# Dilated attention with keys and copied queries held by position class, weights' sums from a ones column

## The chip, the cores and the metric

One core of a Trainium2 chip runs the whole program. The metric is the device time of one execution in microseconds, the median of several runs. TensorE is called PE here (its weight loads PEld), VectorE DVE, ScalarE ACT, GpSimd POOL, and SyncE, which issues the DMAs, SP.

## The reference, cut to what matters

Two transformer blocks follow each other on one sequence of 1024 positions of width 1024. The change lies in the second block's dilated attention: 8 heads of 64 values. Three branches of a softmax over a window of keys are mixed by their denominators, which is one softmax over the keys of all three with those of several branches counted once for each.

```python
DILATED_BRANCHES = ((128, 1), (512, 4), (2048, 16))
...
def dilated_attention(q, k, v, rel_bias):
    outs, lses = [], []
    for window, dil in DILATED_BRANCHES:
        o, l = dilated_window_branch(q, k, v, rel_bias, window, dil)
        ...
    w = jax.nn.softmax(jnp.stack(lses, axis=0), axis=0)
    return jnp.einsum('ibsh,ibshd->bshd', w.astype(q.dtype), jnp.stack(outs, axis=0))
```

The kernel joins the branches with dilation 4 and 16: all their keys have the query's position modulo 4. That is the class piece; the window of dilation 1 is the band piece.

## The kernel before, in words

Values are float32; a matmul operand is split into a high and a low part, and a product is made as high by high, low by high and high by low. In the second block the stages follow each other: values and gates, then the qk stage (queries and keys), then 16 class pieces, then 16 band pieces, and from the fourteenth band piece on the groups of the output projection (`wp_group`).

**The qk stage.** `d_run` makes each block product and hands it to `qk_evac` with its number p and one of four head pairs s. Order of p: 2, 1, 5, 6, 3, 7, 4. Pieces 1 and 4 are the first and second half of the queries, 3 and 7 of the keys; 2, 5, 6 are partial products. `key_operand` (L1239) stores a head pair's keys from an SBUF tile f: ACT casts the high parts (L1247), DVE subtracts for the low ones (L1250), ACT casts a second copy (L1251); positions lie one after another. `query_operand` (L1225) does the same for queries by ACT L1233 and DVE L1236, for piece 4 out of PSUM.

**A piece.** `dil_quad` (L1805) is a generator for four heads and 128 queries. It makes scores (`scores`: four matmuls of 128 rows at L1263, four of 64 at L1268), takes the minimum of bias minus score per query on DVE (L1831) and the exponential on ACT with its sum read out (L1834); after a yield it transposes (PE L1842) and copies out of PSUM (ACT L1845, DVE L1847); after another it multiplies by the values (L1861) and copies the result out (DVE L1863). A class piece (class c, query half qb) reads queries and keys with a step of 4 elements and stores its result, minima and sums into `cls_d` in DRAM. A band piece loads that back (`xc`, L1822) and joins the two by minima and sums (DVE L1870 to L1876, ACT L1872, POOL L1877 to L1881), then transposes the result (PE L1887) and splits it (ACT L1889, DVE L1890).

**What sets the order.** Each `pump` starts one new generator and then steps the older ones, the youngest first. So PE does the scores of piece k, the transposes of k-1 and the products with the values of k-2. Each engine works in program order. `self.low = nc.gpsimd` puts the splits of the output weights (`wl`, L281) on POOL during the band stage. Values for the class pieces (`vc`, four DMAs), for the band (`vb`, nine) and the band's bias (`bb`, two) are loaded on SP between the stages, and each DMA waits for the one eight before it.

Of the kernel before, what the change touches and what calls it, by code (L numbers as in the profile page):

```python
# [10 lines left out]
F32 = mybir.dt.float32  # L11
F32R = mybir.dt.float32r
AF = mybir.ActivationFunctionType
# [162 lines left out]
class Kern:  # L176
# [1062 lines left out]
    def key_operand(self):  # L1239

        nc = self.nc
        k = [self.S("kst", dt=F32R) for _ in range(3)]
        def put(h, ps):
            sl = slice(512 * h, 512 * h + 512)
# [9 lines left out]
    def scores(self, sc, qs, ks, q0, k0, step, nk):  # L1254


        nc = self.nc
        qc = slice(q0 % 512, q0 % 512 + step * (P - 1) + 1, step)
        kc = slice(k0, k0 + step * (nk - 1) + 1, step)
        th = q0 // 512  # L1260
        for j in range(2):
            for s in range(2):
                nc.tensor.matmul(sc[s][:, 256 * j : 256 * j + nk], qs[j][th][:, s, qc], ks[j][s][:, kc],  # L1263
                                 start=(j == 0), stop=False, skip_group_check=True)
        for j in range(2):
            for s in range(2):
                pr = slice(64 * s, 64 * s + 64)
                nc.tensor.matmul(sc[s][:, 256 * j : 256 * j + nk], qs[j][th][pr, s, qc], ks[j][2][pr, kc],  # L1268
                                 start=False, stop=(j == 1), skip_group_check=True)


    def att1_quad(self, n, u, aq, ak, av, att):
# [6 lines left out]
        self.scores(sc, aq[2 * u : 2 * u + 2], [ak, ak], n * P, k0, 1, nk)  # L1279
# [168 lines left out]
    def block2(self, Z, x2_d):  # L1448
# [75 lines left out]
        def vc_load(c):  # L1524
            t = self.S("vc", [P, 2, 512])
            nc.sync.dma_start(t, vsrc[c].rearrange("(b p) c -> p b c", p=P))
            vc.append(t)

        vc, cb = [], []
        cls_d = dp.tile([SEQ, 2, 264], F32, name="cls_d")  # L1530
        qs, ks, kput = [None] * 4, [None] * 4, [None] * 4
        qput = [None] * 4
        cls = [self.dil_quad("c", (c, qb), u, qs, ks, vc, cb, cls_d)
# [3 lines left out]
        def qk_evac(p, s, ps):  # L1537
            th, ch = self.OUT[p]
            if p in (2, 5, 6):
                nc.scalar.copy(self.part(p, s), ps)  # L1540
                return
            src = ps
            if p != 4:
                src = self.H("f")
                nc.vector.tensor_tensor(src, ps, self.part(p, s), ALU.add)
            if ch == 0:
                if p == 1:
                    qs[s], qput[s] = self.query_operand()
                qput[s](th, src)
            else:  # L1550
                if p == 3:
                    ks[s], kput[s] = self.key_operand()
                kput[s](th, src)
            if p == 7 and s == 0:
                vc_load(0)
                cb.extend(self.bias_load(0, 384, "cb", range(4)))
            if p == 4 and s == 0:
                for c in range(1, 4):
                    vc_load(c)
            if p == 4 and s == 3:  # L1560
                self.pend.extend(cls)
# [5 lines left out]
        cb += self.bias_load(0, 384, "cb", range(4, 8))  # L1567

# [3 lines left out]
        vb = [self.S("vb", [P, 2, 512]) for _ in range(5)]  # L1572
        for m in range(9):
            lo, hi = max(0, P * m - 64), min(SEQ, P * m + 64)
            nc.sync.dma_start(vb[m // 2][0 : hi - lo, m % 2, :], v_d[lo:hi, :])
        bb = self.bias_load(L_CLS, 256, "bb")
        while self.pend:
            self.pump()

# [225 lines left out]
    def dil_quad(self, kind, where, u, qs, ks, vt, bias, cls_d, MX=None):  # L1805

        nc = self.nc
        if kind == "c":
            c, qb = where
            q0, k0, step, nk, b0 = c + 512 * qb, c, 4, 256, 128 - 128 * qb  # L1810
            segs = [(0, P, vt[c][:, 0, :]), (P, P, vt[c][:, 1, :])]
            co = self.H("co", [P, 264])
        else:
            n = where
            lo, hi = max(0, P * n - 64), min(SEQ, P * n + 192)
            q0, k0, step, nk, b0 = n * P, lo, 1, hi - lo, lo - (P * n - 64)
            segs = []
            for m in (n, n + 1):
                a0, a1 = max(0, P * m - 64), min(SEQ, P * m + 64)
                segs.append((a0 - lo, a1 - a0, vt[m // 2][0 : a1 - a0, m % 2, :]))  # L1820
            x2 = self.S("xc", [P, 2, 264])
            nc.sync.dma_start(x2[:, 0, :], cls_d[n * P : n * P + P, u, :])  # L1822
            co = x2[:, 1, :]
        sc = [self.PS("sc") for _ in range(2)]
        self.scores(sc, qs[2 * u : 2 * u + 2], ks[2 * u : 2 * u + 2], q0, k0, step, nk)
        z = self.S("z", [P, 4, 256])
        for s in range(2):
            for j in range(2):
                h, x = 4 * u + 2 * j + s, 2 * j + s
                nmc = co[:, 256 + x : 257 + x]  # L1830
                nc.vector.tensor_tensor_reduce(  # L1831
                    out=z[:, x, :nk], in0=sc[s][:, 256 * j : 256 * j + nk], in1=bias[h][:, b0 : b0 + nk], scale=-0.125,
                    scalar=BIG, op0=ALU.add, op1=ALU.min, accum_out=nmc)
                nc.scalar.activation(z[:, x, :nk], z[:, x, :nk], AF.Exp, bias=nmc, scale=-1.0,  # L1834
                                     accum_out=co[:, 260 + x : 261 + x])
        yield
        pT = self.S("pT", [P, 8, P])
        for g in range(2):
# [4 lines left out]
            if kind == "c" or segs[0][1] == segs[1][1]:  # L1843
# [14 lines left out]
        for x in range(4):  # L1858
            h = 4 * u + x
            for e, (o, w, vv) in enumerate(segs):  # L1860
                nc.tensor.matmul(pv[:, 64 * x : 64 * x + 64], pT[0:w, 2 * x + e, :], vv[:, 64 * h : 64 * h + 64],  # L1861
                                 start=(e == 0), stop=(e == 1))
# [5 lines left out]
        d, e = (self.mp.tile([P, 2, 4], F32, tag="d2", name=self.nm("d2"), bufs=6) for _ in range(2))  # L1868
        mn, rc = self.M("mn", 4), self.M("rc", 4)
        nc.vector.tensor_tensor(mn, x2[:, 0, 256:260], x2[:, 1, 256:260], ALU.min)  # L1870
        nc.vector.tensor_tensor(d, mn[:, None, :].to_broadcast([P, 2, 4]), x2[:, :, 256:260], ALU.subtract)
        nc.scalar.activation(e, d, AF.Exp)  # L1872
        yield
        nc.vector.tensor_tensor(d, e, x2[:, :, 260:264], ALU.mult)
        nc.vector.tensor_tensor(rc, d[:, 0, :], d[:, 1, :], ALU.add)
        nc.vector.reciprocal(rc, rc)  # L1876
        nc.gpsimd.tensor_tensor(e, e, rc[:, None, :].to_broadcast([P, 2, 4]), ALU.mult)  # L1877
        for i in range(2):
            v = x2[:, i, 0:256].rearrange("p (h d) -> p h d", d=64)
            nc.gpsimd.tensor_tensor(v, v, e[:, i, :, None].to_broadcast([P, 4, 64]), ALU.mult)  # L1880
        nc.gpsimd.tensor_tensor(co[:, 0:256], co[:, 0:256], x2[:, 0, 0:256], ALU.add)  # L1881
        yield
# [3 lines left out]
        for j in range(2):  # L1886
            nc.tensor.transpose(tp[:, j, :], co[:, P * j : P * j + P], self.ident)  # L1887
        hi, lo = (z[:, :, (n % 4) * P : (n % 4) * P + P] for z in MX.pair(u, n // 4))
# [35 lines left out]
```

## Time and profile before

| | us |
|---|---|
| median of 3 runs (lowest to highest) | 2574.4 (2571.2 to 2575.66) |
| the profiled execution's own time | 2574.72 |
| its span | 2572.9 |
| busy PE / DVE / ACT / POOL in the span | 2504.7 / 1765.6 / 1142.2 / 178.7 |
| qk stage ends, class stage, band stage (start to end in the span) | 1681; 1683.7 to 1756.5; 1756.5 to 1861 |

Times of a trace row count from the start of the span. Busy shares are averages over stages with different limits; what bounds a stretch is read from the chain of waits in it.

### The profile page before, as it was taken

How to read it: one execution, taken by the hardware profiler on the slowest of the kernel's cores; microseconds unless marked ns; L12 is line 12 of the kernel's file. 1: busy time of each engine (PE TensorE's matmuls, PEld its weight loads, DVE VectorE, ACT ScalarE, POOL GpSimd, SP SyncE). 2: the span in 40 equal slices, each digit the busy share in tenths (PEclk: the TensorE clock that was granted, in tenths of full speed). 3: DMA queues.
4: the chain of work that ended last, by engine and by line, in shares of the span. 5: the costliest groups of instructions: out<-in, count | busy, mean ns of one | idle time of the engine just before them, and what ended most of it. 6: DMA issues, size and time to landing. Idle time of an engine off the chain costs nothing.

```text
span 2572.9 us, 31324 instructions
## 1 busy us (share of the span) xinstructions
PE 2504.7 (97%) x11857; PEld 2073.0 (81%) x11857; DVE 1765.6 (69%) x2789; ACT 1142.2 (44%) x2068; POOL 178.7 (7%) x236
## 2 busy tenths in 40 slices
PE   7999999999999999999999999999999999899998
PEld 5888888888787888878788777888887888788886
DVE  7664456556899755555799986666558444478888
ACT  5444445412425433333333644566436555553334
POOL 1000000000002000000000300002421000000006
PEclk9999999999999999999999999999899999999999
DMA  4333333135343122233433415221242333522334
GB/s 157 104 110 103 123 103 107 39 113 185 109 186 131 66 70 87 87 130 98 174 121 131 144 49 172 102 81 51 81 160 82 104 117 103 180 108 81 115 123 147
DMA packets 178703, 291.57 MB, mean 113 GB/s; under 512 B 10168, under 2 KB 84552, under 8 KB 178552
## 3 DMA queue, kind: packets, MB, share of 16 engines
q1 hardware_dynamic: 178552, 289.57, 33.1%
q8 instruction: 93, 1.52, 0.2%
q14 instruction: 58, 0.48, 0.1%
HBM read 212.89 MB, written 80.31 MB: 114 GB/s over the span
## 4 chain that ended last, share of the span: by engine, by line
PE 78%; DVE 13%; DMA 3%; ACT 3%; issue 2%; POOL 1%; SPq 0%; DVEq 0%; ACTq 0%; POOLq 0%
PE da L1201 6%; PE a L500 6%; PE a L502 6%; PE a L501 6%; PE da L1200 6%; PE da L1199 6%; PE db L1201 3%; PE db L1200 3%; PE db L1199 3%; PE b L502 3%; PE b L501 3%; PE b L500 3%; DVE wl L281 3%; PE pv L1861 2%; DVE midl L281 2%
## 5 line engine op out<-in xcount | busy, mean ns | idle before, releaser
L500 PE MATMUL a<-midh,ws 128*128 128x512 f32 x708 | 276.8, 391 | 9.1 <-DVE f L1669 8.0
L502 PE MATMUL a<-midh,ws 128*128 128x512 f32 x708 | 276.4, 390 | 0.0
L501 PE MATMUL a<-midl,ws 128*128 128x512 f32 x708 | 276.4, 390 | 0.0
L1201 PE MATMUL da<-wh,midl 128*128 128x512 f32 x624 | 245.1, 393 | 6.6 <-DVE midl L281 6.6
L1200 PE MATMUL da<-wl,midh 128*128 128x512 f32 x624 | 244.6, 392 | 3.4 <-DVE wl L281 3.4
L1199 PE MATMUL da<-wh,midh 128*128 128x512 f32 x624 | 246.0, 394 | 0.6 <-ACT midh L279 0.6
L279 ACT CAST midh<-mt 128x1024 fp32r<-128x1024 f32 x80 | 82.9, 1036 | 244.6 <-DVE mt L1142 81.3
L1201 PE MATMUL db<-wh,midl 128*128 128x512 f32 x436 | 171.0, 392 | 3.5 <-DVE midl L281 3.5
L1200 PE MATMUL db<-wl,midh 128*128 128x512 f32 x436 | 170.8, 392 | 2.2 <-DVE wl L281 2.2
L1199 PE MATMUL db<-wh,midh 128*128 128x512 f32 x436 | 171.1, 392 | 1.4 <-ACT midh L279 1.4
L500 PEld LDWEIGHTS a<-midh,ws 128*128 128x128 f32 x708 | 133.4, 188 | 38.7 <-issue 8.9
L501 PEld LDWEIGHTS a<-midl,ws 128*128 128x128 f32 x708 | 133.5, 189 | 27.7
L502 PEld LDWEIGHTS a<-midh,ws 128*128 128x128 f32 x708 | 133.5, 189 | 27.7
L279 ACT CAST ws<-tc 128x512 fp32r<-128x512 f32 x180 | 111.4, 619 | 88.3 <-DVE tc L414 87.1
L1201 PEld LDWEIGHTS da<-wh,midl 128*128 128x128 f32 x624 | 117.8, 189 | 34.5 <-DVE midl L281 10.3
L1200 PEld LDWEIGHTS da<-wl,midh 128*128 128x128 f32 x624 | 117.9, 189 | 29.0 <-DVE wl L281 4.8
L500 PE MATMUL b<-midh,ws 128*128 128x512 f32 x360 | 140.1, 389 | 0.0
L501 PE MATMUL b<-midl,ws 128*128 128x512 f32 x360 | 140.1, 389 | 0.0
L502 PE MATMUL b<-midh,ws 128*128 128x512 f32 x360 | 140.0, 389 | 0.0
L279 ACT CAST wh<-raw 128x1024 fp32r<-128x1024 f32 x121 | 120.6, 1037 | 42.0 <-DMA raw<-in_w_ff_dram 15.2
L1199 PEld LDWEIGHTS da<-wh,midh 128*128 128x128 f32 x624 | 118.0, 189 | 26.0 <-issue 1.2
L281 DVE TENSOR_TENSOR wl<-raw,wh 128x1024 fp32r<-128x1024 f32 x117 | 136.2, 1197 | 3.6 <-ACT wh L279 3.5
(348 smaller groups left out, 5822.8 us busy)
## 6 DMA issues: line engine op xcount, KB each, us to landing
raw<-in_w_ff_dram SPq DMA_DIRECT2D x31, 1024.0 KB, 5.4
mid_d<-f SPq DMA_DIRECT2D x108, 256.0 KB, 2.1
midr<-mid_d SPq DMA_DIRECT2D x52, 512.0 KB, 6.9
raw<-in_w_in_dram SPq DMA_DIRECT2D x22, 1024.0 KB, 5.4
x<-x_d SPq DMA_DIRECT2D x24, 512.0 KB, 4.5
raw<-in_w_up_dram SPq DMA_DIRECT2D x11, 1024.0 KB, 5.6
raw<-in_w_gate_dram SPq DMA_DIRECT2D x10, 1024.0 KB, 5.5
xt<-in_x_dram SPq DMA_DIRECT2D x16, 512.0 KB, 10.9
```

The source lines that it names most:

```text
L279: self.nc.scalar.copy(hi, s)
L281: e.tensor_tensor(lo, s, hi.bitcast(F32), ALU.subtract)
L500: nc.tensor.matmul(ps, hi[:, i], xh, start=(first and i == 0), stop=False, skip_group_check=True)
L501: nc.tensor.matmul(ps, hi[:, i], xl, start=False, stop=False, skip_group_check=True)
L502: nc.tensor.matmul(ps, lo[:, i], xh, start=False, stop=(i == 3), skip_group_check=True)
L1199: nc.tensor.matmul(ps, xh, wh, start=(kt == 0 and p in (1, 5, 2)), stop=False, skip_group_check=True)
L1200: nc.tensor.matmul(ps, xh, wl, start=False, stop=False, skip_group_check=True)
L1201: nc.tensor.matmul(ps, xl, wh, start=False, stop=(kt == m - 1), skip_group_check=True)
L1861: nc.tensor.matmul(pv[:, 64 * x : 64 * x + 64], pT[0:w, 2 * x + e, :], vv[:, 64 * h : 64 * h + 64], start=(e == 0), stop=(e == 1))
```

## The change

Keys and a second copy of the queries are stored grouped by position modulo 4 (class by class). A class piece then reads both without a step; a band piece reads its 256 keys as eight runs of 32, so its columns stand by class, and its value tiles and bias are brought into that order too. The first and last band piece of each half use two groups of columns instead of one: 16 matmuls instead of 8, 8 minima instead of 4. Each head's 64 values get a 65th column of ones, so that a product with the weights also gives their sum; the exponential no longer reads a sum. A band piece starts its minimum from the class piece's, so the class part is scaled by one exponential and added. The class result's copy out of PSUM moves from DVE to ACT.

```diff
-    def key_operand(self):
+    def key_operand(self, r=1):
...
+            w = 512 // r
+            v = [x.rearrange("p (r j) -> p r j", r=r)[:, :, w * h : w * h + w] for x in k]
+            ps = ps.rearrange("p (j r) -> p r j", r=r)
             for s in range(2):
                 pr = slice(64 * s, 64 * s + 64)
-                nc.scalar.copy(k[s][pr, sl], ps[pr, :])
+                nc.scalar.copy(v[s][pr], ps[pr])
             for s in range(2):
...
-                nc.vector.tensor_tensor(k[2][pr, sl], ps[pr, :], k[s][pr, sl].bitcast(F32), ALU.subtract)
-                nc.scalar.copy(k[s][po, sl], ps[pr, :])
+                nc.vector.tensor_tensor(v[2][pr], ps[pr], v[s][pr].bitcast(F32), ALU.subtract)
+                nc.scalar.copy(v[s][po], ps[pr])
...
+        def vb_load(u, m):
+            lo, hi = max(0, 32 * m - 16), min(256, 32 * m + 16)
+            v, w = v_slot("vb", vb, u, m), hi - lo
+            for c in range(4):
+                nc.sync.dma_start(
+                    v[c * w : c * w + w], vsrc[c, lo:hi, 256 * u : 256 * u + 256].rearrange("p (h d) -> p h d", d=64))
...
                 qput[s](th, src)
+                qc[s][th] = t = self.S("qc", [P, 2, 512], F32R)
+                for i in range(2):
+                    nc.scalar.copy(t[:, i, :].rearrange("p (r j) -> p r j", r=4),
+                                   qs[s][th][:, i, :].rearrange("p (j r) -> p r j", r=4))
...
+            if step == 10:
+                for m in range(9):
+                    vb_load(0, m)
+            if step in (11, 12):
+                h = 4 * (step - 11)
+                b, t = self.bias_load(L_CLS, 256, "bn", range(h, h + 4)), self.S("bb", [P, 4, 256])
+                for i in range(4):
+                    nc.gpsimd.tensor_copy(t[:, i, :].rearrange("p (g r j) -> p g r j", g=2, r=4),
+                                          b[i].rearrange("p (g j r) -> p g r j", g=2, r=4))
...
+                if i == 4:
+                    for m in range(9):
+                        vb_load(1, m)
...
             nc.sync.dma_start(x2[:, 0, :], cls_d[n * P : n * P + P, u, :])
+            yield
...
+                nm = co[:, 260 + x : 261 + x]
+                least = BIG if kind == "c" else x2[:, 0, 260 + x : 261 + x]
+                for o, w, fb, fz in parts:
+                    nc.vector.tensor_tensor_reduce(
+                        out=fz(z[:, x, o : o + w]), in0=fz(sc[s][:, 256 * j + o : 256 * j + o + w]), in1=fb(bias[h]),
+                        scale=-0.125, scalar=least, op0=ALU.add, op1=ALU.min, accum_out=nm)
+                    least = nm
+                nc.scalar.activation(z[:, x, :nk], z[:, x, :nk], AF.Exp, bias=nm, scale=-1.0)
+        if kind == "b":
...
+            nc.gpsimd.tensor_tensor(d, co[:, 260:264], x2[:, 0, 260:264], ALU.subtract)
+            nc.scalar.activation(d, d, AF.Exp)
+            v = x2[:, 0, 0:260].rearrange("p (h d) -> p h d", d=65)
+            nc.gpsimd.tensor_tensor(v, v, d[:, :, None].to_broadcast([P, 4, 65]), ALU.mult)
         yield
...
-        nc.vector.tensor_copy(co[:, 0:256], pv[:, 0:256])
         if kind == "c":
+            nc.scalar.copy(co[:, 0:260], pv[:, 0:260])
...
+        nc.vector.tensor_tensor(co[:, 0:260], pv[:, 0:260], x2[:, 0, 0:260], ALU.add)
```

The `vc` loads go from four DMAs of 512 KB to sixteen of 128 KB, eight of them before the class stage; the `vb` loads from nine to 72. In the changed file the exponential is L1891, the copies out of PSUM L1908 and L1926, the query copies L1575, the band's class load L1860, its scale L1895 to L1898.

**ACT where the qk stage ends.** kst and qst are stored keys and queries, qc the copied queries, da the PSUM tile of piece 4. Before:

```order
L1247 CAST kst_12987<-f_13078 64x512
L1247 CAST kst_12988<-f_13078 64x512
L1251 CAST kst_12987<-f_13078 64x512
L1251 CAST kst_12988<-f_13078 64x512
L1233 CAST qst_13098<-da_12670 64x512 x2
L1233 CAST qst_13121<-da_12671 64x512 x2
L1233 CAST qst_13138<-da_12672 64x512 x2
L1233 CAST qst_13155<-da_12673 64x512 x2
L1834 ACT_TABLE_LOAD
L1834 ACTIVATE z_13171,co_13160<-z_13171,co_13160 128x256 x4
```

Changed:

```order
L1233 CAST qst_13113<-da_12670 64x512 x2
L1575 COPY qc_13118<-qst_13113 128x512 x2
L1233 CAST qst_13142<-da_12671 64x512 x2
L1575 COPY qc_13147<-qst_13142 128x512 x2
L1233 CAST qst_13162<-da_12672 64x512 x2
L1575 COPY qc_13167<-qst_13162 128x512 x2
L1233 CAST qst_13182<-da_12673 64x512 x2
L1575 COPY qc_13187<-qst_13182 128x512 x2
L1891 ACT_TABLE_LOAD
L1891 ACTIVATE z_13201<-z_13201,co_13190 128x256 x4
```

Two copies qc now stand behind each pair of casts, ahead of the table load for the exponential and of the first exponential.

**SP where the band stage begins.** cls_d is the stored class result, xc a band piece's load of it, v_d the values in DRAM, sgr an input of the output projection. Before:

```order
L1822 DMA xc_13899<-cls_d 128x264
L1865 DMA cls_d<-co_13807 128x264
L1822 DMA xc_13946<-cls_d 128x264
L1822 DMA xc_13997<-cls_d 128x264
L1822 DMA xc_14055<-cls_d 128x264
L1822 DMA xc_14113<-cls_d 128x264
L1822 DMA xc_14174<-cls_d 128x264
L1822 DMA xc_14239<-cls_d 128x264
L1791 DMA sgr_14306<-sgu_d_11488 128x512
```

Changed:

```order
L1860 DMA xc_13962<-cls_d 128x264
L1927 DMA cls_d<-co_13889 128x264
L1860 DMA xc_14010<-cls_d 128x264
L1860 DMA xc_14050<-cls_d 128x264
L1860 DMA xc_14101<-cls_d 128x264
L1548 DMA vb_14152<-v_d 16x4x64 x4
L1548 DMA vb_14152<-v_d 32x4x64 x8
L1548 DMA vb_14166<-v_d 32x4x64 x12
L1548 DMA vb_14180<-v_d 32x4x64 x8
L1548 DMA vb_14180<-v_d 16x4x64 x4
L1860 DMA xc_14194<-cls_d 128x264
```

Thirty-six loads of vb stand between the fifth and the sixth load xc; as many more stand before the last class results.

## Rows read from the trace of the kernel before

**Rows 1.** the page: its span, and the busy time of each engine

```profile
span 2572.9 us, 31324 instructions
...
PE 2504.7 (97%) x11857; PEld 2073.0 (81%) x11857; DVE 1765.6 (69%) x2789; ACT 1142.2 (44%) x2068; POOL 178.7 (7%) x236
```

**Rows 2.** table by stretches: busy time per engine, granted clock, DMA

```profile
1640.00:1655.00 15.00, 15.00 (x68) 12.43 (x67) 6.00 (x6) 7.58 (x12) 0.00 (x0) 1.00 0.21 70
1655.00:1681.00 26.00, 26.00 (x117) 21.52 (x116) 19.24 (x26) 20.50 (x34) 0.00 (x0) 1.00 0.71 245
1696.50:1756.50 60.00, 60.00 (x417) 54.24 (x418) 32.42 (x130) 32.66 (x117) 0.00 (x0) 1.00 0.09 31
1800.00:1820.00 20.00, 18.89 (x111) 16.52 (x111) 16.26 (x52) 13.37 (x45) 14.59 (x15) 0.74 0.29 101
```

**Rows 3.** chain of waits, class stage: start us, duration us, what

```profile
1696.48 1.10 PE sc L1263 x4
1697.58 0.77 PE sc L1268 x4
1698.34 1.02 PE tp L1842 x8
1699.37 1.73 PE pv L1861 x16
...
1756.54 0.48 PE sc L1263 x4
```

**Rows 4.** chain of waits, first band pieces

```profile
1760.17 0.52 PE sc L1263 x4
1760.70 0.43 PE sc L1268 x4
```

**Rows 5.** timeline of DVE, end of qk: start us, us, engine, line, operation

```profile
1674.92 0.69 DVE L1545 TENSOR_TENSOR f<-da,yp 128x512 f32<-128x512 f32 x1
1676.30 1.40 DVE L1250 TENSOR_TENSOR kst<-f,kst 64x512 fp32r<-64x512 f32 x2 [0.69 <-ACT kst L1247]
1677.73 0.69 DVE L1545 TENSOR_TENSOR f<-da,yp 128x512 f32<-128x512 f32 x1
...
1682.10 5.66 DVE L1236 TENSOR_TENSOR qst<-da,qst 64x512 fp32r<-64x512 f32 x8 [1.60 <-ACT qst L1233]
```

**Rows 6.** timeline of ACT, same stretch

```profile
1675.64 1.26 ACT L1247 CAST kst<-f 64x512 fp32r<-64x512 f32 x2 [0.26 <-DVE f L1545]
...
1680.90 4.76 ACT L1233 CAST qst<-da 64x512 fp32r<-64x512 f32 x8
1685.68 1.28 ACT L1834 ACT_TABLE_LOAD   x1
1688.26 0.51 ACT L1834 ACTIVATE z<-z,co 128x256 f32<-128x256 f32 x1 [1.30 <-DVE co L1831]
```

**Rows 7.** the page, costliest groups: busy us, mean ns of one

```profile
L279 ACT CAST midh<-mt 128x1024 fp32r<-128x1024 f32 x80 | 82.9, 1036 | 244.6 <-DVE mt L1142 81.3
...
L279 ACT CAST ws<-tc 128x512 fp32r<-128x512 f32 x180 | 111.4, 619 | 88.3 <-DVE tc L414 87.1
```

**Rows 8.** groups by form, class stage: count, busy us, mean ns of one

```profile
L1847 DVE COPY pT<-tp 128x512 f32<-128x512 f32 x13 | 8.9, 686 | 0.0
...
L1863 DVE COPY co<-pv 128x256 f32<-128x256 f32 x13 | 5.5, 424 | 8.5 <-PE pv L1861 8.5
```

**Rows 9.** timeline of DVE, band stage

```profile
1801.05 2.28 DVE L1874 TENSOR_TENSOR d<-d,xc 128x8 f32<-128x8 f32 x1
1803.36 2.26 DVE L1875 TENSOR_TENSOR rc<-d 128x4 f32<-128x4 f32 x1
```

**Rows 10.** timeline of POOL, same stretch

```profile
1800.93 4.67 POOL L281 TENSOR_TENSOR wl<-raw,wh 128x1024 fp32r<-128x1024 f32 x2
```

**Rows 11.** timeline of SP's DMA queue, band stage

```profile
1764.80 13.35 SPq L1822 DMA_DIRECT2D xc<-cls_d  x6
...
1785.90 0.43 SPq L1791 DMA_DIRECT2D sgr<-sgu_d  x1
```

More of the change, by code (lines that the diff above doesn't have):

```diff
@@ L1278, in att1_quad @@
         sc = [self.PS("sc") for _ in range(2)]
-        self.scores(sc, aq[2 * u : 2 * u + 2], [ak, ak], n * P, k0, 1, nk)
+        qo = n * P % 512
+        self.scores(sc, aq[2 * u : 2 * u + 2], [ak, ak], lambda t: t[n * P // 512][:, :, qo : qo + P],
+                    [(0, nk, lambda t: t[:, k0 : k0 + nk])])
         z = self.S("z", [P, 4, 256])
@@ L1567, in block2 @@
         cb += self.bias_load(0, 384, "cb", range(4, 8))
+        for i in range(8):
+            vc_load(1, i)
         MX = MixAct(self, "mx", 8)
@@ L1571, in block2 @@
         MX.expect(("s", t) for t in range(NT))
[L1572 to L1576, printed above, removed]
+        bb, step = [], 0
         while self.pend:
             self.pump()
+            step += 1
+            if step == 10:
[7 more added lines that the diff above has]
+                                          b[i].rearrange("p (g j r) -> p g r j", g=2, r=4))
+                    bb.append(t[:, i, :])
         ys = []
@@ L1809, in dil_quad @@
             c, qb = where
-            q0, k0, step, nk, b0 = c + 512 * qb, c, 4, 256, 128 - 128 * qb
-            segs = [(0, P, vt[c][:, 0, :]), (P, P, vt[c][:, 1, :])]
+            q = lambda t: t[qb][:, :, P * c : P * c + P]
+            keys = [(0, 256, lambda t: t[:, 256 * c : 256 * c + 256])]
+            segs = [(e * P, P, vt[u, 2 * c + e]) for e in range(2)]
+            parts = [(0, 256, lambda b: b[:, 128 - 128 * qb : 384 - 128 * qb], lambda z: z)]
             co = self.H("co", [P, 264])
@@ L1814, in dil_quad @@
             n = where
[L1815 to L1820, printed above, removed]
             x2 = self.S("xc", [P, 2, 264])
             nc.sync.dma_start(x2[:, 0, :], cls_d[n * P : n * P + P, u, :])
+            yield
             co = x2[:, 1, :]
+            q0 = P * (n % 4)
+            q = lambda t: t[n // 4][:, :, q0 : q0 + P]
+            k0, cut, k1 = max(0, 32 * n - 16), 32 * n + 16, min(256, 32 * n + 48)
+            segs = [(0, 4 * (cut - k0), vt[u, n]), (4 * (cut - k0), 4 * (k1 - cut), vt[u, n + 1])]
+            by_class = lambda t: t.rearrange("p (r j) -> p r j", r=4)
+            if k1 - k0 == 64:
+                keys = [(0, 256, lambda t: by_class(t)[:, :, k0:k1].rearrange("p r (g j) -> p g r j", g=2))]
+                parts = [(0, 256, lambda b: b, lambda t: t)]
+            else:
+                keys = [(o, w, lambda t, lo=k0 + o // 4, w=w: by_class(t)[:, :, lo : lo + w // 4]) for o, w, _ in segs]
+                parts = [(o, w, lambda b, e=e, at=(k0 + o // 4 + 16 - 32 * n) % 32, w=w:
+                          by_class(b[:, P * e : P * e + P])[:, :, at : at + w // 4], by_class)
+                         for e, (o, w, _) in enumerate(segs)]
         sc = [self.PS("sc") for _ in range(2)]
-        self.scores(sc, qs[2 * u : 2 * u + 2], ks[2 * u : 2 * u + 2], q0, k0, step, nk)
+        self.scores(sc, qs[2 * u : 2 * u + 2], ks[2 * u : 2 * u + 2], q, keys)
         z = self.S("z", [P, 4, 256])
+        nk = sum(w for _, w, _ in segs)
         for s in range(2):
@@ L1842, in dil_quad @@
                     nc.tensor.transpose(tp[0:w, 2 * x + e, :], z[:, 2 * g + x, o : o + w], self.ident)
-            if kind == "c" or segs[0][1] == segs[1][1]:
+            if segs[0][1] == segs[1][1]:
                 if g == 0:
@@ L1858, in dil_quad @@
         for x in range(4):
-            h = 4 * u + x
             for e, (o, w, vv) in enumerate(segs):
-                nc.tensor.matmul(pv[:, 64 * x : 64 * x + 64], pT[0:w, 2 * x + e, :], vv[:, 64 * h : 64 * h + 64],
+                nc.tensor.matmul(pv[:, 65 * x : 65 * x + 65], pT[0:w, 2 * x + e, :], vv[0:w, 65 * x : 65 * x + 65],
                                  start=(e == 0), stop=(e == 1))
-        nc.vector.tensor_copy(co[:, 0:256], pv[:, 0:256])
         if kind == "c":
+            nc.scalar.copy(co[:, 0:260], pv[:, 0:260])
             nc.sync.dma_start(cls_d.rearrange("(j r) u c -> r j u c", r=4)[c, P * qb : P * qb + P, u, :], co)
             return
[L1868 to L1882, printed above, removed]
+        nc.vector.tensor_tensor(co[:, 0:260], pv[:, 0:260], x2[:, 0, 0:260], ALU.add)
+        sums = co[:, 0:260].rearrange("p (h d) -> p h d", d=65)
+        rc = self.M("rc", 4)
+        nc.vector.reciprocal(rc, sums[:, :, 64])
+        y = x2[:, 0, 0:256]
+        nc.gpsimd.tensor_tensor(y.rearrange("p (h d) -> p h d", d=64), sums[:, :, 0:64],
+                                rc[:, :, None].to_broadcast([P, 4, 64]), ALU.mult)
         yield
@@ L1886, in dil_quad @@
         for j in range(2):
-            nc.tensor.transpose(tp[:, j, :], co[:, P * j : P * j + P], self.ident)
-        hi, lo = (z[:, :, (n % 4) * P : (n % 4) * P + P] for z in MX.pair(u, n // 4))
+            nc.tensor.transpose(tp[:, j, :], y[:, P * j : P * j + P], self.ident)
+        hi, lo = (z[:, :, q0 : q0 + P] for z in MX.pair(u, n // 4))
         nc.scalar.copy(hi, tp[:, 0:2, :])
```

59 lines of the change are left out of this document (31 added, 28 removed).

## The prediction

> **What bounds the kernel now.** The page comes first: PE is busy 2504.7 us of a span of 2572.9 [rows 1], so time goes only where PE's own work shrinks or where PE waits. The profiled execution took 2574.72 us, 0.3 above the median of 2574.4. About 0.2%, 5 us, is what a measurement of this kernel can tell from no change. The change acts on one stretch, from the queries' and keys' storing (from about 1622) to the end of the band pieces (1861).
>
> I read that stretch next as a table of stretches [rows 2]. The reader is to see that PE is busy through all 26 us from 1655 to 1681 and all 60 us from 1696.5 to 1756.5, while DVE and ACT use little over half of the latter; and that PE has a clock of 0.74 and some idle time in 1800 to 1820. Then the chain of waits says what one class piece is: scores 1.10 and 0.77, transposes 1.02, products 1.73, all PE [rows 3]. From 1696.48 to 1756.54 are 13 such pieces: 4.62 each. A band piece has the same matmuls, but its keys and queries are read without a step, and its scores take 0.52 and 0.43 [rows 4]. So a step of four elements makes PE's scores 1.87 instead of 0.95, 1.96 times. Last I read the timelines of DVE and ACT where the qk stage ends [rows 5, 6], since the change moves the stepped reads there.
>
> **What it gains.** Class scores fall to 0.95, the band's price, since both operands are then contiguous as there. A piece is then 3.71, and 13 pieces give 13 x 0.91 = **-11.8 us**. PE stays the bound: ACT's 32.66 us over 13 pieces [rows 2] are 2.5 each, and the copy that moves to it adds at most DVE's 0.42 [rows 8], together 2.9; DVE's 2.5 falls by as much.
>
> **What it adds before the first class piece.** The key's three stores now read f with a step of four on ACT (two casts and two copies a head pair) and on DVE (two subtractions), and there are 16 new stepped copies of 128x512 on ACT. No row of before shows such a read on ACT or DVE. The bounds: free, or PE's 1.96 times on the part that grows with the columns. That part: on ACT 1024 columns cost 1.036 and 512 cost 0.619 [rows 7], so 0.42 of 0.62 is by the column; on DVE 686 and 424 ns for 512 and 256 columns [rows 8] leave 0.53 by the column and 0.16 fixed. A 512-column read is so 0.62 to 1.02 on ACT and 0.69 to 1.20 on DVE. I take 1.6 times, 0.87 and 1.01: nearer to PE's row than to nothing, since the step is the same, but below it, since PE asks for a column in 0.51 ns where ACT asks in 0.81 and DVE in about 1.02, and the slower reader has less to lose.
>
> [...]
>
> *Keys.* The period of a store is DVE's chain: f 0.69, the wait for ACT's first cast 0.69, the subtractions 1.40, from 1674.92 to 1677.73 2.8 [rows 5]; ACT waits 0.26 each time [rows 6], and PE has no idle time beside it [rows 2]: at 2.8 the store just keeps up with PE, and what it grows by is no longer covered. With the prices taken it is 0.69 + 0.87 + 2.02 = 3.6. Eight stores (pieces 3 and 7) make 8 x 0.8 = 6.4 us later, and the last ends at 1687.4, not 1681.
>
> *Copied queries of piece 1.* Four pairs of copies, some 7 us of ACT in all. ACT is idle for half of 1640 to 1655 [rows 2], and so I cost them at nothing; without that cover, 7 us.
>
> *Copied queries of piece 4.* Today ACT casts for 4.76 us without a pause, the table load follows, and the first exponential starts at 1688.26 [rows 6]. Now two copies stand behind each pair of casts on ACT, and each waits for DVE's subtraction, whose first starts 1.2 after the casts do [rows 5, 6]. Per head pair: casts 1.19, wait 0.76, copies 1.74, together 3.7; four make 14.8, and with the load 1.28 the first exponential comes at 1687.4 + 16.1 = 1703.5: **+15.2 us**. Free reads would give 1.19 + 0.76 + 1.24 = 3.2 a pair, 1681 + 12.8 + 1.3 = 1695.1: +6.8. PE's ratio gives 4.1 a store and 4.0 a pair: 1691.4 + 17.3 = 1708.7: +20.4. Scores, the first minima and the first exponentials follow each other as now, behind it.
>
> So the class stage ends 15.2 - 11.8 = +3.4 us later (-5.0 with free reads, +8.6 with PE's ratio).
>
> **The band stage.** Four edge pieces make their scores by 16 matmuls instead of 8; a 64-column one costs 0.11 (1.73 for 16, rows of the products [rows 3]), so 16 are 1.7 instead of 0.9: at most +0.8 each, and I take half, +1.8 in all. The 65th column adds 1/64 of 1.73 in 32 pieces: +0.9. What goes: DVE's small two-operand steps, which stretch to 2.28 and 2.26 us while POOL splits the output weights for 4.67 [rows 9, 10]; PE then waits and falls to a clock of 0.74 [rows 2]. I take 4.5 for the two and 1.5 for half of the clock's loss: -6. What is late next: SP issues 36 loads of vb between the fifth and the sixth xc, at 0.43 each [rows 11] 15.5 us, and the sixth piece's minimum now waits for its xc. Today six xc loads go out from 1764.80 to 1778.15, far ahead of need [rows 11]; then the sixth would issue 15.5 behind the fifth, near 1767 + 15.5 = 1782.5, while its piece, which the added yield puts one turn later, makes its minimum near 1756.5 + 6 x 3.7 + 0.95 = 1779.7. The turn of transposes and products in between hides about half of what is late with the load's landing: +2, between 0 and 6. Exponential, reads without sums and bias copies on POOL lie beside PE. Sum of the band: **-1.3 us**.
>
> **Forecast.** 2574.7 + 3.4 - 1.3 = 2576.8, less the 0.3 by which this execution stood above the median: 2576.5. No change that a measurement can tell.
>
> **The rivals.**
> *Free or nearly free reads.* ACT and DVE ask for less than the pace that PE still gets through the step (256 columns in 0.27, 1.07 ns each [rows 3]), so they could see nothing. For it: that pace is close to DVE's own. Then 2574.4 - 5.0 - 1.3 = 2568, and 2566 if the sixth xc is in time: faster.
> *PE's ratio holds.* [...] The first exponential after 1707 decides.
> *The band's new waits.* The minimum waits for xc, and ACT, which works in order, waits with the exponential of d for POOL's subtraction, which stands behind the weight splits of 4.67 [rows 10]. From the point where POOL takes a split before a piece's subtraction, ACT's later exponentials stand behind it, and PE idles and slows as in 1800 to 1820 now [rows 2]. The 6 us aren't saved, the sixth xc costs its 6: 2576.5 + 6 + 4 = 2587, slower. Against it: most pieces meet no split.
> *The scores don't shrink.* If their 1.87 comes from the queries' weight loads or from the output and not from the stepped keys, the class piece stays 4.62 and 2576.5 + 11.8 = 2588 follows. Against it: the band piece differs in the step alone [rows 3, 4].
>
> **How the numbers follow.** Forecast 0.38 (2571 to 2582: 0.05 faster, 0.26 the same, 0.07 slower); free reads 0.32 (0.27 faster, 0.05 the same); PE's ratio 0.13 (0.10 slower); the band's waits 0.12 (0.10 slower); scores unchanged 0.05 (0.04 slower). Together faster 0.32, the same 0.37, slower 0.31. The range reaches from 2563, below the free reads by the band's uncertainty, to 2588; 0.8 of the cases lie in it. The forecast's own range is 2571 to 2582.
>
> **What would show it.** In the changed profile: class scores of 0.52 and 0.43 and a piece of 3.7; casts of keys between 0.8 and 0.95 and copies of queries alike; the first exponential between 1700 and 1707; no small DVE step over 1 us in the band. Casts at 0.62 and the exponential near 1695 show the first rival, casts over 1.0 the second, a wait of ACT for POOL or of DVE for xc of over 3 us the third. I am wrong too if PE fills the gap before the first class piece with other work, or if the band stage, 104.5 us long, changes by more than 6.

## The result and the profile after

The changed kernel takes 2604.4 us (2603.98 to 2609.55, four runs); the kernel before has a median of 2574.4 in three runs (2571.2 to 2575.66). A fourth run of the kernel before took 4680.04 us and is left out of the ratio. The ratio is 1.0127, 95% interval 1.0114 to 1.0139: **slower by 1.3%**, outside the range of the prediction (by the medians alone 30.0 us, 1.2%). The profiled execution has a span of 2602.5 us, 29.6 more than before.

The two profiled executions are already 1.4 us apart where the changed stretch begins, at ACT's first cast of the queries of piece 1. So the stages are compared below by times counted from this cast in the same execution; "from the first cast" means this. The products are a piece's multiplications by the values (L1861, in the changed kernel L1923). From the timelines of ACT and PE, the first cast and the products of class piece 14 and of band piece 1, before and then changed:

```profile
1622.09 1.26 ACT L1233 CAST qst<-f 64x512 fp32r<-64x512 f32 x2 [1.02 <-DVE f L1545]
...
1754.64 1.90 PE L1861 MATMUL pv<-vc,pT 128*128 128x64 f32 x16
...
1765.77 2.98 PE L1861 MATMUL pv<-vb,pT 64*128 64x64 f32 x16
```

```profile
1620.67 1.26 ACT L1233 CAST qst<-f 64x512 fp32r<-64x512 f32 x2 [1.02 <-DVE f L1567]
...
1764.85 1.90 PE L1923 MATMUL pv<-vc,pT 128*128 128x65 f32 x16
...
1788.94 2.98 PE L1923 MATMUL pv<-vb,pT 64*128 64x65 f32 x16
```

| us from the first cast to | before | changed | changed is later by |
|---|---|---|---|
| the first exponential | 66.17 | 89.44 | 23.3 |
| the products of class piece 14 | 132.6 | 144.2 | 11.6 |
| the products of band piece 1 | 143.7 | 168.3 | 24.6 |
| the products of band piece 8 | 170.7 | 199.5 | 28.8 |
| the products of band piece 16 | 232.8 | 267.9 | 35.1 |
| the end of the program | 950.8 | 981.8 | 31.0 |

What was to be won was won. The chain of waits of the changed kernel, class stage (start us, duration us, what):

```profile
1718.42 0.53 PE sc L1265 x4
1718.95 0.43 PE sc L1271 x4
1719.39 1.03 PE tp L1905 x8
1720.41 1.73 PE pv L1923 x16
1722.15 0.53 PE sc L1265 x4
...
1744.45 0.53 PE sc L1265 x4
```

A class piece is 3.72 instead of 4.62 [rows 3]: seven from 1718.42 to 1744.45 take 26.03. The scores are at the band's old price [rows 4]. In the table the lag falls from 23.3 to 11.6 over the class pieces.

It was lost at two places. The first is the end of the qk stage. The timelines of ACT and of DVE in the changed kernel (start us, us, engine, line, operation, count, idle before and who ended it):

```profile
1664.14 2.24 ACT L1250 CAST kst<-f 64x512 fp32r<-64x512 f32 x2
1666.40 2.22 ACT L1254 CAST kst<-f 64x512 fp32r<-64x512 f32 x2
1668.64 2.21 ACT L1250 CAST kst<-f 64x512 fp32r<-64x512 f32 x2
...
1690.58 2.18 ACT L1254 CAST kst<-f 64x512 fp32r<-64x512 f32 x2
...
1694.58 2.09 ACT L1575 CAST qc<-qst 128x512 fp32r<-128x512 f32 x2 [0.75 <-DVE qst L1236]
1696.68 1.17 ACT L1233 CAST qst<-da 64x512 fp32r<-64x512 f32 x2
...
1708.82 1.28 ACT L1891 ACT_TABLE_LOAD   x1
1710.11 2.11 ACT L1891 ACTIVATE z<-z,co 128x256 f32<-128x256 f32 x5
```

```profile
1663.01 0.69 DVE L1567 TENSOR_TENSOR f<-db,yp 128x512 f32<-128x512 f32 x1
1665.27 2.19 DVE L1253 TENSOR_TENSOR kst<-f,kst 64x512 fp32r<-64x512 f32 x2 [1.58 <-ACT kst L1250]
```

A cast of keys out of f takes 1.12 instead of 0.63 [rows 6], a subtraction 1.10 instead of 0.70 [rows 5], a copy of queries 1.05. A key store takes 4.50 (1664.14 to 1668.64) instead of 2.81, the last cast ends at 1692.76, and four head pairs of piece 4 follow at 4.03 each. The first exponential starts at 1710.11, **21.85 later** than before [rows 6], or 23.3 counted from the first cast.

The second place is the end of the class stage and the band stage. SP's queue there, and the minimum of DVE that waited longest:

```profile
1748.98 18.35 SPq L1548 DMA_DIRECT2D vb<-v_d  x36
1767.44 0.36 SPq L1927 DMA_DIRECT2D cls_d<-co  x1
...
1783.26 1.35 SPq L1860 DMA_DIRECT2D xc<-cls_d  x3
1784.71 16.97 SPq L1548 DMA_DIRECT2D vb<-v_d  x36
1801.78 1.32 SPq L1860 DMA_DIRECT2D xc<-cls_d  x3
```

```profile
1769.38 0.42 DVE L1887 CUSTOM_DVE_ANT_0 z<-sc,cb 128x256 f32<-128x256 f32 x1 [6.91 <-DMA cls_d<-co]
```

The first 36 loads of vb hold SP for 18.35 us. The class results of 1752 and after wait behind them to be stored; each holds one of its pool's six buffers (`co`); a later piece's minima are written into such a buffer, and waited 6.91 us for the store that frees it. The second 36 hold SP for 16.97 us, and the sixth xc goes out at 1801.78; its landing is on the chain for 4.11 us. The table of stretches shows PE at the end of the qk stage, at the first wait, behind it, and later in the band stage (length, busy time of PE, PEld, DVE, ACT, POOL with their instructions, granted clock, DMA share, GB/s):

```profile
1655.00:1681.00 26.00, 20.88 (x87) 16.48 (x87) 17.48 (x20) 22.90 (x22) 0.00 (x0) 0.97 0.41 112
1764.00:1772.00 8.00, 4.23 (x30) 3.69 (x31) 2.07 (x9) 2.15 (x6) 0.00 (x0) 0.75 0.55 147
1772.00:1796.00 24.00, 24.00 (x124) 21.66 (x122) 10.58 (x47) 9.95 (x29) 8.01 (x16) 0.59 0.42 122
1820.00:1850.00 30.00, 29.27 (x133) 25.19 (x131) 14.73 (x62) 14.96 (x39) 17.32 (x21) 0.54 0.37 119
```

At the first wait PE idles 3.77 of 8 us, and then works 24 us without a pause at a mean granted clock of 0.59: 0.50 in the 15 us from 1772 to 1787 and 0.73 in the 9 behind them. A piece's products take longer there, in the chain:

```profile
1772.75 3.31 PE pv L1923 x16
...
1778.81 3.60 PE pv L1923 x16
```

Before, at a granted clock of 1.00, they took 1.73 [rows 2, 3]. Later PE works 30 us at 0.54; this stretch begins some 16 us behind the wait for xc, and what set it off is not shown. Before, the slow stretch was 1800 to 1820 [rows 2]. In the 26 us before 1681 PE now idles 5, where it had none [rows 2].

### The profile page after: what moved, and what is told of

Same layout as the page of the kernel before. It is cut to its first block, busy times and chain, and to the rows that moved or that the text cites. A ratio compares the mean times of both kernels' runs of the same rounds, so it can differ in the third digit from the quotient of the medians.

```text
span 2602.5 us, 31366 instructions
## 1 busy us (share of the span) xinstructions
PE 2510.0 (96%) x11889; PEld 2077.2 (80%) x11889; DVE 1756.1 (67%) x2753; ACT 1168.6 (45%) x1972; POOL 173.4 (7%) x228
## 4 chain that ended last, share of the span: by engine, by line
PE 73%; DVE 14%; DMA 5%; ACT 5%; issue 2%; SPq 1%; POOL 1%; DVEq 0%; ACTq 0%; POOLq 0%
PE a L500 6%; PE a L502 6%; PE a L501 6%; PE da L1201 5%; PE da L1200 5%; PE da L1199 5%; DVE wl L281 3%; PE db L1201 3%; PE db L1200 3%; PE db L1199 3%; PE b L501 3%; PE b L502 3%; PE b L500 3%; DVE midl L281 2%; PE pv L1923 2%
```

## The experiments

All times are medians of several runs, with the kernel before run beside them; its median moved from 2572.2 to 2574.9 between the experiments. The ratios are to it, with their 95% intervals. A difference to the changed kernel, which was measured beside other runs, is uncertain by some 3 us.

**1. The price of the stepped read.** Stepped reads made contiguous, the instructions left as they are.

```diff
-            ps = ps.rearrange("p (j r) -> p r j", r=r)
+            ps = ps.rearrange("p (r j) -> p r j", r=r)
...
-                                   qs[s][th][:, i, :].rearrange("p (j r) -> p r j", r=4))
+                                   qs[s][th][:, i, :].rearrange("p (r j) -> p r j", r=4))
```

> The changed kernel with the stepped reads of the keys' stores and of the query copies made contiguous; the number and size of the instructions stay, the keys and copied queries are then in the wrong order. Theory (price of the read): casts fall from 1.11 to 0.62, subtractions from 1.10 to 0.69, copies from 1.06 to 0.62, a key store from 4.5 to 2.8, and the first exponential from 1710.1 to about 1695: 14 to 16 us less, near 2589. Rival (order on ACT): what delays the first class piece is that the copies stand in ACT's order between the casts and the exponential and wait for DVE, whatever they cost: the first exponential stays after 1704 and the time falls by 6 or less.

Measured: 2587.49, ratio 1.0056 (1.0039 to 1.0073), 17 below the changed kernel. The groups of ACT (shapes, count, busy us, mean ns of one), of the changed kernel and then of this one:

```profile
L1254 ACT CAST kst<-f 64x512 fp32r<-64x512 f32 x16 | 17.6, 1098 | 0.3
...
L1575 ACT CAST qc<-qst 128x512 fp32r<-128x512 f32 x8 | 8.4, 1100 | 3.0 <-DVE qst L1236 3.0
```

```profile
L1254 ACT CAST kst<-f 64x512 fp32r<-64x512 f32 x16 | 9.9, 619 | 0.3
...
L1575 ACT CAST qc<-qst 128x512 fp32r<-128x512 f32 x8 | 4.9, 618 | 3.6 <-DVE qst L1236 3.5 <-DVE vc L1533 0.2
```

The theory holds: casts 0.62, copies 0.62, and the first exponential starts at 1694.41, 73.56 from the first cast (1620.85 here) instead of 89.44. The price, not the order alone, delayed the class stage: of the 23.3 us, 15.9 are the price, and 7.4, by which this exponential is still behind the one before the change, are the order.

**2. The order of the stepped read, once instead of six times.** DVE writes f by class, the six instructions that read f are contiguous.

```diff
-            ps = ps.rearrange("p (j r) -> p r j", r=r)
+            ps = ps.rearrange("p (r j) -> p r j", r=r)
...
-                nc.vector.tensor_tensor(src, ps, self.part(p, s), ALU.add)
+                dst = src.rearrange("p (r j) -> p j r", r=4) if ch else src.rearrange("p (j r) -> p j r", r=4)
+                nc.vector.tensor_tensor(dst, ps.rearrange("p (j r) -> p j r", r=4),
+                                        self.part(p, s).rearrange("p (j r) -> p j r", r=4), ALU.add)
```

> The changed kernel with the keys' order made once: DVE writes the sum f by class (a stepped write of 512 columns), and the six reads of f per head pair are contiguous. Theory: a stepped write costs as a stepped read, f takes 1.1 instead of 0.69, the casts and subtractions fall to 0.62 and 0.69, a store takes 3.2 instead of 4.5, eight stores 10 us less, and the last key cast ends near 1683 instead of 1692.8: 8 to 11 us less, near 2595. Rival: a stepped write costs more than a read (over 2 us), and nothing is gained: within 2 of the changed kernel.

Measured: 2590.69, ratio 1.0071 (1.0056 to 1.0086), 14 below the changed kernel. DVE's timeline:

```profile
1659.44 1.09 DVE L1568 TENSOR_TENSOR f<-db,yp 128x512 f32<-128x512 f32 x1
1661.22 1.40 DVE L1253 TENSOR_TENSOR kst<-f,kst 64x512 fp32r<-64x512 f32 x2 [0.69 <-ACT kst L1250]
```

DVE's stepped write costs what its stepped read did, 1.09 against 0.69 without a step (the read 1.10), and pays for six. A store takes 3.2, and the table load comes at 1696.75. The gain is larger than expected. The table load is 12 us earlier, but counted from the first cast (1618.89 here) 10.3, inside the 8 to 11 expected: 1.8 us lie ahead of the changed stretch, and the rest is within the uncertainty named above.

**3. The query copies off ACT.** All 16 on POOL.

```diff
-                    nc.scalar.copy(t[:, i, :].rearrange("p (r j) -> p r j", r=4),
+                    nc.gpsimd.tensor_copy(t[:, i, :].rearrange("p (r j) -> p r j", r=4),
```

> The changed kernel with the 16 stepped query copies on POOL instead of ACT. Theory: behind piece 4 ACT casts for 4.8 us as before the change, the table load follows, and the first exponential comes near 1699 instead of 1710.1, since the first four class pieces need only the copies of piece 1: 9 to 12 us less, 2592 to 2595; a POOL copy of 128x512 takes 1.1 us (the bias copies: 0.6 for 256 columns). Rival: POOL's copies stretch DVE's subtractions of two SBUF operands, as POOL's splits stretched small DVE steps to 2.3 us in the kernel before, and the class pieces wait for POOL: 3 us less or none.

Measured: 2598.0 (2592.94 to 2601.33), ratio 1.0096 (1.0081 to 1.0111), 6 below the changed kernel. ACT's timeline:

```profile
1693.27 4.75 ACT L1233 CAST qst<-da 64x512 fp32r<-64x512 f32 x8
1698.04 1.28 ACT L1891 ACT_TABLE_LOAD   x1
1700.75 1.71 ACT L1891 ACTIVATE z<-z,co 128x256 f32<-128x256 f32 x4 [1.43 <-DVE co L1887]
```

The casts stand together again and the table load comes 10.8 earlier, as the theory has it; but the first exponential, which now waits for DVE's minima, is only 7.9 earlier from the first cast (1619.23 here), and some 6 us reach the end, between the two expectations. POOL's copies of piece 1 take back 2.0 of it: from the first cast to the first cast of keys it is 34.65 instead of 32.64. The loads of vb stand at the same piece as in the changed kernel and still hold the stores.

**4. 18 band loads instead of 72.** The ones stand beside the values in DRAM, in rows of 520, so that a value tile is one DMA of 1040-byte runs.

```diff
-            for c in range(4):
-                nc.sync.dma_start(
-                    v[c * w : c * w + w], vsrc[c, lo:hi, 256 * u : 256 * u + 256].rearrange("p (h d) -> p h d", d=64))
+            nc.sync.dma_start(
+                v[0 : 4 * w], bass.AP(tensor=v_d.tensor, offset=v_d.offset + 2080 * lo + 260 * u,
+                                      ap=[[520, 4], [2080, w], [1, 260]]))
```

> The changed kernel with the values stored in DRAM together with their ones column, rows of 520, so that a value tile of the band is one DMA of 1040-byte runs instead of four of 256-byte runs: 18 DMAs instead of 72, and no memsets beside them. Theory (SP's queue): the 36 loads that held the queue for 18.35 us from 1748.98 kept class results from being stored, their buffers from coming free, and the next minimum waited 6.91 us; the second 36 made the sixth class load late by 4. With 9 loads of some 4 to 5 us in each place both waits go, and with them the half clock that follows: 12 to 18 us less than the changed kernel, 2586 to 2592, no DMA wait over 1 us in the chain of the class stage. Rival (the band's own new work): the edge matmuls, the minimum's wait for its load and the chain through POOL hold the band back whatever SP does: at most 4 us less, 2600 or more, and PE's half clock stays in 1820 to 1850.

Measured: 2590.36, ratio 1.0069 (1.0054 to 1.0084), 14 below the changed kernel. SP's timeline, and the loads of xc left in the chain of waits:

```profile
1749.58 8.86 SPq L1549 DMA_DIRECT2D vb<-v_d  x9
...
1778.91 8.41 SPq L1549 DMA_DIRECT2D vb<-v_d  x9
```

```profile
1787.42 6.63 DMA xc<-cls_d
...
1811.04 4.97 DMA xc<-cls_d
...
1830.00 4.82 DMA xc<-cls_d
```

The theory's time holds, and the wait for a store's buffer is gone. Its detail does not: nine loads in a row still hold SP for 8.9 and 8.4 us, twice what was expected, and three loads of xc are late.

**5. 72 loads, but four to a piece.** This parts the place in the queue from the shortness of the runs.

```diff
-            if step == 10:
-                for m in range(9):
-                    vb_load(0, m)
+            if 6 <= step < 15:
+                vb_load(0, step - 6)
...
-                if i == 4:
-                    for m in range(9):
-                        vb_load(1, m)
+                if 2 <= i < 11:
+                    vb_load(1, i - 2)
```

> The changed kernel with its 72 band loads kept as they are, but issued four to a piece instead of 36 in a row at two places. Theory (a row of loads ahead of the class stores on SP's queue): four loads hold SP for about 2 us, less than a piece of 3.7, so the wait of 6.91 us for a class store's buffer goes, and the time falls nearly as with 18 loads, 10 to 16 us below the changed kernel: 2588 to 2594. Rival (the 256-byte runs themselves, as work of the DMA engines): spreading them changes nothing, 2600 or more.

Measured: 2588.71, ratio 1.0060 (1.0043 to 1.0077), 16 below the changed kernel. SP's timeline:

```profile
1741.24 0.34 SPq L1925 DMA_DIRECT2D cls_d<-co  x1
1741.62 1.88 SPq L1548 DMA_DIRECT2D vb<-v_d  x4
1744.96 0.34 SPq L1925 DMA_DIRECT2D cls_d<-co  x1
```

Four loads hold SP for 1.88, a store goes out every 3.7, and the time falls as much as with 18 loads. It is the rows of 36 loads, not the 256-byte runs. The edit parts both rows at once, but the trace tells them apart: from the products of class piece 14 to those of band piece 1 it is 12.9 us here, 24.1 in the changed kernel, 11.1 before; from band piece 1 to 8 it is 28.6 here, 31.2 in the changed kernel. The first row, ahead of the class stores, costs 11.2 and the second 2.6.

**6. The gain alone.** The kernel before, its class pieces reading without a step; their results then belong to other positions.

```diff
-            q0, k0, step, nk, b0 = c + 512 * qb, c, 4, 256, 128 - 128 * qb
+            q0, k0, step, nk, b0 = 128 * c + 512 * qb, 256 * c, 1, 256, 128 - 128 * qb
```

> The kernel before with nothing changed but that the class pieces read the stored queries and keys without a step (128 adjacent queries, 256 adjacent keys; their results then belong to other positions). Theory: the step alone makes the class scores 1.87 instead of 0.95, 13 pieces and the three before gain 11 to 14 us, 2560 to 2563, which is what the change could have won. Rival (the gain is given back at the next wait: class stores, loads, or the band's first pieces): less than 6 us.

Measured: 2560.72, ratio 0.9947 (0.9933 to 0.9962): 14 us below the kernel before. PE's groups in the class stage:

```profile
L1263 PE MATMUL sc<-kst,qst 128*128 128x256 f32 x41 | 7.4, 300 | 0.0
L1268 PE MATMUL sc<-kst,qst 64*128 64x256 f32 x44 | 5.5, 330 | 0.0
```

All of the gain reaches the end of the program. Queries and keys lose their step together here, so which of the two makes the price is not shown.

**7. The repairs together.** First 2, 3 and 4 in one kernel.

> The three repairs together: values stored with their ones column (18 band loads), query copies on POOL, keys ordered once in f. Theory: the three causes lie one behind the other and add. The last key cast ends near 1680.6, the first exponential comes near 1688 as in the kernel before; 13 class pieces gain 11.8 us; the band keeps the 4 to 5 us that it is longer than before in the run with 18 loads: 6 to 9 us faster than the kernel before, near 2566. Rival (they overlap, or the earlier class stage only waits longer for SP): the loads of the class stage's stores and values now bind earlier, and the time stays at the kernel before's or above, 2572 or more.

Measured: 2573.91, ratio 0.9998 (0.9988 to 1.0007): no change, the rival's time. The timelines of DVE and POOL at piece 1 show one cost that neither expectation had:

```profile
1624.81 4.03 DVE L281 TENSOR_TENSOR wl<-wt,wh 128x1024 fp32r<-128x1024 f32 x2
...
1634.13 1.81 DVE L1236 TENSOR_TENSOR qst<-f,qst 64x512 fp32r<-64x512 f32 x2 [0.74 <-ACT qst L1233]
```

```profile
1624.19 3.56 POOL L1579 CAST qc<-qst 128x512 fp32r<-128x512 f32 x2 [55.69 <-DVE qst L1236]
...
1638.63 3.60 POOL L1579 CAST qc<-qst 128x512 fp32r<-128x512 f32 x2 [0.68 <-DVE qst L1236]
```

Beside POOL's copies two weight splits take 4.03 instead of 2.36 and two subtractions 1.81 instead of 1.40. This costs 2.1 us: from the first cast to the first cast of keys it is 35.12 here and 33.03 in the run with f by class alone, whose copies are on ACT. The class stage gained what it should: the products of class piece 14 come 7.2 earlier than before, from the first cast. The band stage loses it again: from the products of band piece 1 to those of piece 16 it is 97.1 us, where the kernel before has 89.1. The chain from 1741 on holds a load of the band's bias (bn, 7.90 us) and four loads of xc, 4.22 to 6.95 us each.

Then the splits of the output weights back on DVE in the band stage, the loads spread as in 5, and both.

```diff
-        self.low = nc.gpsimd
+        self.low = nc.vector
```

> The same with the splits of the output weights back on DVE in the band stage. Theory: POOL's splits of 2.36 us hold the raw weight buffers, the load of the next raw weights stands at the head of SP's queue, and the class loads xc behind it come late (4.97 and 4.82 us of the chain in the run with 18 loads). On DVE a split takes 1.2 us, the raw load goes out earlier: 4 to 8 us less than with the three repairs alone. Rival: DVE is what the band waits for, four splits of 1.2 us in its order delay minima and copies: 0 to 4 us more.

> The three repairs with the 18 band loads spread, one to a piece, instead of nine in a row at two places. Theory: nine in a row still hold SP for 8.4 to 8.9 us and make the sixth class load late (6.63 us of the chain in the run with 18 loads); spread, each waits beside the others: 3 to 6 us less than with the three repairs alone. Rival: the wait of the sixth load is its own buffer's or its landing's, and nothing changes by more than 2.

> The three repairs, splits on DVE and loads spread. Theory: both band waits are gone, the half clock behind them too: 14 to 20 us faster than the kernel before, 2552 to 2558. Rival: one takes the other's place, and the sum is no better than the better of the two.

Measured: splits on DVE 2569.39, ratio 0.9990 (0.9975 to 1.0005), no clear change; loads spread 2569.72, 0.9986 (0.9977 to 0.9995); both 2566.49, 0.9972 (0.9961 to 0.9982). Alone each is near the small end of the theory, with an interval that overlaps that of the three repairs, and both together are half of theirs; two loads of xc (4.11 and 4.87 us) are still in the last one's chain. The traces say more of the splits: from the products of band piece 8 to those of piece 16 it is 68.1 us with the three repairs and 60.8 with the splits on DVE, 65.8 with the loads spread and 61.4 with both.

Last, the copies of piece 1 back on ACT and those of piece 4 left on POOL; then cb and vc loaded earlier as well; then one more yield behind the load of xc.

```diff
-                    nc.gpsimd.tensor_copy(t[:, i, :].rearrange("p (r j) -> p r j", r=4),
+                    (nc.scalar.copy if p == 1 else nc.gpsimd.tensor_copy)(t[:, i, :].rearrange("p (r j) -> p r j", r=4),
```

```diff
-                cb.extend(self.bias_load(0, 384, "cb", range(4)))
-            if p == 4 and s == 0:
+            if p == 3 and s == 2:
+                cb.extend(self.bias_load(0, 384, "cb", range(4)))
+            if p == 7 and s == 2:
                 for i in range(3, 8):
```

```diff
             nc.sync.dma_start(x2[:, 0, :], cls_d[n * P : n * P + P, u, :])
             yield
+            yield
```

> The last kernel (three repairs, splits on DVE, loads spread) with the query copies of piece 1 back on ACT and only those of piece 4 on POOL. Theory: on POOL the piece-1 copies ran beside DVE's weight splits and stretched two of them from 2.36 to 4.03 us in all, and PE idled near 1640; on ACT they hide in its idle time, and everything from there on is 3 to 4 us earlier: 2562 to 2564. Rival: ACT's copies delay its casts there by as much, and nothing changes by more than 1.

> The same with the bias of the class pieces and the later value loads issued earlier in the qk stage. Theory: the chain before the first class piece shows waits for the loads of cb (4.25 us) and vc (2.2 to 2.7 us); issued earlier they are off the chain: 1 to 3 us less than the run before it in this call. Rival: ACT's table load ends last there anyway, and nothing changes.

> The same with one more yield between a band piece's class load and its scores, so that SP has one more piece's time for it. Theory: the two xc waits still in the chain (4.11 and 4.87 us, with the half clock behind them) go: 4 to 8 us less than the run before it in this call. Rival: the loads wait for a free buffer, not for SP's turn, and an earlier place in the order changes nothing, or the extra buffer held makes another load late: 0 to 4 us more.

Measured: 2565.01, ratio 0.9966 (0.9954 to 0.9977); 2562.99, 0.9960 (0.9946 to 0.9974); 2564.5, 0.9966 (0.9954 to 0.9979). The intervals overlap, so the times show none of the three steps by itself. In the traces the first exponential comes 71.05 from the first cast with all copies on POOL and 69.0 in each of these three: the first step is worth 2.1, less than the 3 to 4 expected, and the earlier loads of cb and vc move the first exponential by nothing, their rival. The extra yield brought nothing either: the rival. The second of them, 0.4% faster than the kernel before, has the lowest median of the kernels that compute what the reference does, 2 to 3 us from the 2560.72 that the unstepped scores alone give. Its chain of waits still has these loads:

```profile
1790.32 4.62 DMA xc<-cls_d
...
1802.08 5.37 DMA xc<-cls_d
```

What holds them there is not shown.

## Why the prediction was wrong

**"13 x 0.91 = -11.8 us"**: right. The piece is 3.72, the lag falls by 11.7 from the first exponential to class piece 14, and alone the step is worth 14 us (experiment 6). That PE stays the bound is right too.

**"I take 1.6 times, 0.87 and 1.01"**: too small. ACT's read costs 1.10 on the mean (experiment 1), 2.1 times on the part by the column ((1.10 - 0.20) / 0.42), above PE's 1.96; DVE's subtraction 1.10, 1.8 times on its 0.53. The argument that a slower reader has less to lose is what failed. With the fixed parts that the prediction took off, PE through the step gets a column in 1.07 ns, ACT gets one in (1.10 - 0.20) / 512 = 1.76 ns and DVE in (1.10 - 0.16) / 512 = 1.84. With contiguous reads the working itself was good: it had the first exponential at 1695.1, and experiment 1 has 1694.41.

**"0.69 + 0.87 + 2.02 = 3.6"** a store: 4.50. With the dearer casts the bound is ACT, four casts of 1.1 on one engine, and not DVE's chain. From the first cast, the end of the last key cast came 13.2 us later where 6.4 were foreseen, a head pair of piece 4 takes 4.03 where 3.7 were foreseen, and the first exponential was 23.3 later instead of 15.2. The rival with PE's ratio had 20.4, and with it 2574.4 + 8.6 - 1.3 = 2582 for the whole; why ACT and DVE lose about what PE does is not shown. That piece 1's copies cost nothing is right: from the first cast to the first cast of keys (1653.31) it is 32.64 us in both kernels.

**"Sum of the band: -1.3 us"**: this is the step that failed most. At class piece 14 the lag is 11.6 and at the end 31.0, so the way from there to the end cost 19.4 instead of gaining 1.3. I costed the second 36 loads of vb at +2, near the 2.6 measured, and the first 36 at nothing, although their place ahead of the last class stores stood in the order. A store was not on any path before; with 18 us of loads ahead of it six buffers are not enough. The first row costs 11.2, and spreading all 72 loads takes 15.7 us away (experiment 5). The cost is more than the wait: the wait was 6.9 us, and behind it PE worked 24 us at a granted clock of 0.59. From 1750 to 1800 the mean granted clock is 0.76 in the changed kernel and 0.97 in experiment 5, where that wait is gone.

The term of -6, the saving on DVE's small steps, failed as well: no run shows it. From the products of band piece 1 to those of piece 16 the kernel before takes 89.1 us, the changed kernel 99.6, the one with spread loads 95.2, and the best one 90.4. What holds the band stage of the changed kernel back there, apart from the rows, is only in part known.

The rival with the band's new waits named POOL's splits as the mechanism, and the loads of vb only by the sixth xc. It had a part: its sign, a wait of DVE for xc of over 3 us, was there with 4.0, and from band piece 8 to 16 the five kernels with the splits on DVE take 60.8 to 62.9 where the changed kernel and the seven others made from it with the splits on POOL take 65.2 to 70.1 (the kernel before, also on POOL, 62.0). But it was not ACT waiting for POOL: no POOL step of a microsecond stands in the changed kernel's chain from 1700 to 1900. And the largest cost, the first row, it had not.

The first rival, free reads, is refuted by experiment 1; its premise fails on the rows of before as well, since a contiguous column, worked out from them at 0.81 ns for ACT and 1.02 for DVE [rows 7, 8], comes faster than PE's 1.07 through the step [rows 3]. That the scores don't shrink is refuted by experiment 6.

## What to carry to other kernels

A stepped layout was paid here where it is made as well as where it is read (DVE's write 1.09 instead of 0.69, ACT's read 1.10 instead of 0.62): make it once, in one instruction, and let every other reader be contiguous; the stepped reads on the path to the first exponential cost 15.9 us, more than the 14 that the stepped matmuls gave up. Where a change adds transfers, look at every store and load that stands behind them on the same queue, count the buffers that these hold, and price the row of them against that: here 18.35 us of loads stood against six buffers. Look at the granted clock behind a wait too: here a wait of 6.9 us, with 24 us of PE's work at 0.59 behind it, came to some 11.

## What was not expected of the hardware

A read of 512 float32 columns with a step of four elements took ACT 1.10 instead of 0.62 us and DVE 1.10 instead of 0.69; a write with such a step took DVE 1.09. ACT, faster on contiguous columns, was no faster than DVE on these. Beside POOL's copies of 128x512 DVE's instructions with two SBUF operands took up to 1.7 times as long (4.03 instead of 2.36 for two), and POOL's own copies 3.56 for two; beside DVE's subtractions out of PSUM eight of them took 8.47, 1.06 each, and the subtractions, which read one operand out of PSUM, 5.73 against 5.66 before [rows 5]. Why the two engines slow each other in the one case and hardly in the other is not shown.
